# Second MLP's down projection: seven half-size block products per 1024-row group in place of eight

## The chip, the core and the metric

The kernel runs on one core of a Trainium2 chip. The core has five engines that work side by side, each through its own instructions in a fixed order: TensorE (PE in the profile, with PEld for the loading of its stationary operand), VectorE (DVE), ScalarE (ACT), GpSimd (POOL) and SyncE (SP, which here only issues transfers). They wait for each other by semaphores. Sixteen DMA engines move data between the device's memory and the on-chip memory; they are told what to do through queues that SP, ACT or POOL fill.

The metric is the time of one execution on the device, in microseconds (us). The time before is 1501.96 us, the median of three runs (1501.39 to 1502.55). The profile is one further execution, recorded instruction by instruction.

## What is computed

The reference is a two-layer decoder trunk over 512 positions of width 1024, in float32. A layer is a token mixer (a gated delta rule in the first, a convolution module in the second), a cross-attention, and an MLP. The change touches the MLP of the second layer and the final norm behind it; w_up is 1024 x 4096 and w_down 4096 x 1024:

```python
def sq_relu_mlp(h, w_up, w_down):
    return jnp.square(jax.nn.relu(h @ w_up)) @ w_down
...
        h = h + sq_relu_mlp(rms_norm(h, mlp_norm[layer]), mlp_w_up[layer], mlp_w_down[layer])
    return rms_norm(h, final_norm)
```

## The kernel before

Every projection runs in three passes: an operand x is split into a rounded part xh and the rest xl = x - xh, both of type float32r (fp32r in the profile), and a product is xh·wh + xl·wh + xh·wl (`mm3`, lines 236 to 240). One matmul instruction has a stationary operand of 128x128 and a moving one of 128x512.

**Weights.** They are read in halves of 128x1024, 512 KB each, in one long list (`order`) laid down beforehand for the whole kernel by `plan`. `wload` (line 197) issues the next half on SP's queue into a buffer `raw` (3 of them); `wsplit` (line 205) makes `wh` on ScalarE (line 214) and `wl` on VectorE (line 69, called from line 219), into 3 buffers each (`NW`); `wnext` (line 226) keeps loads and splits ahead of the use and hands out the next half. A third buffer of `wh` comes free when TensorE has finished the half three before. So the split of a half can run while TensorE works on the two halves before it.

**The MLP** (`mlp`, line 1008) goes through `MLP_ORDER`: up projections of 1024 hidden channels ("up", g) and down projections of the same channels ("dn", g), g from 0 to 3, the down projection one group behind the up projection. A step of either kind is 8 output tiles, each 24 matmuls (8 contraction tiles, three passes) on one weight half, into one of 8 PSUM banks. After an up tile VectorE makes `rl` (line 72: relu and the norm's factor), ScalarE squares it (line 1018) and `split` (line 275) makes `uh` and `ul`. After a down tile VectorE adds the bank to the running residual `h`. Activations lie with channels on the partitions, so `h` has 8 tiles of 128 channels x 512 positions.

**The last group** of the second MLP is done otherwise (`finish`, line 1497): for each of 4 blocks of 128 positions and each half of the channels one bank takes four transposes of the residual (line 1507) and 24 matmuls with the weights as the moving operand (lines 1510 to 1512), so that the output comes out with positions on the partitions. The final norm follows bank by bank: a square with a sum (ACT, line 1514), for the second half of a row block a square root (ACT, line 1523), a reciprocal (DVE, line 1524), a scaling of the first half (ACT, line 1525) and of the second (DVE, line 1526, profile line 72), and the two stores.

In the second layer's convolution GpSimd adds up taps (`cb`) and makes some `wl` itself, and VectorE runs a long series of taps over tiles `x7`, which lie in a pool `fsp` of 3 buffers of 128x1024.

Of the kernel before, what the change touches and what calls it, by code (L numbers as in the profile page):

```python
# [8 lines left out]
F32 = mybir.dt.float32  # L9
# [28 lines left out]
def tile_trunk(ctx, tc, xT, memT, x_d, mem_d, prm_d, adt_d, bdw_d, tap_d, fin_d, w_ab, w_kq, w_v, w_z, w_dno, w_pw1, w_pw2,  # L38
# [13 lines left out]
    def nm(s):  # L52
        cnt[0] += 1
        return f"{s}_{cnt[0]}"
# [4 lines left out]
    def psum(s="ps"):  # L59
        return psp.tile([P, NT], F32, tag="ps", name=nm(s))  # L60
# [42 lines left out]

    raw0 = wp.tile([P, 1024], F32, tag="raw", name="raw0", bufs=NRAW)

# [38 lines left out]

    order, srcs = [], {}

    def plan(key, src, n=2):
        srcs[key] = src
        for hf in range(n):
            order.append((key, hf))  # L150

# [12 lines left out]

    def plan_mlp(layer, last=False):
        for kind, g in MLP_ORDER:
            if last and (kind, g) == ("dn", 3):
                break
# [16 lines left out]
    for kind, i in CONV_SEQ:  # L185
        if kind == "p":
            order.append((("pw1", i // 2), i % 2))
        elif kind == "k":
            order.append((("K", 1, i // 2) if i < 8 else ("V", 1, i // 2 - 4), i % 2))
    for i in range(4):  # L190
        plan(("pw2", i), w_pw2[i])
    plan_x(1)
    plan_mlp(1, True)

    ws = {"next": 0, "split": 0, "load": 1, "raw": {0: raw0}, "hl": {}}

    def wload():
        u = ws["load"]
        key, hf = order[u]
        ws["load"] += 1  # L200
        raw = wp.tile([P, 1024], F32, tag="raw", name=nm("raw"), bufs=NRAW)
        nc.sync.dma_start(out=raw, in_=srcs[key][:, hf * 1024:(hf + 1) * 1024])
        ws["raw"][u] = raw

    def wsplit():
        u = ws["split"]
        ws["split"] += 1
        while ws["load"] <= u:
            wload()
        raw = ws["raw"].pop(u)  # L210
        h = wp.tile([P, 1024], F32R, tag="wh", name=nm("wh"), bufs=NW)
        lo = wp.tile([P, 1024], F32R, tag="wl", name=nm("wl"), bufs=NW)
        with tc.issue_after(ws["rb"].ins) if u == 4 else nullcontext():
            ins = [act.copy(h, raw)]  # L214
        if u < 4:
            tc.keep_in_program_order(ins[0])
        (kind, i, *j), hf = order[u]
# [6 lines left out]
        ws["hl"][u] = (h, lo)  # L224

    def wnext(key, hf):
# [7 lines left out]
        return ws["hl"].pop(i)  # L234

    def mm3(ps, wk, xk, first, last):
# [770 lines left out]

    def mlp(layer, norm, hres, nxt, mid=None, end=None, pre=None):
        xs = norm.xs
# [11 lines left out]
        for kind, g in MLP_ORDER:  # L1021
            if (kind, g) == ("dn", 3) and mid is not None:
                mid()
            if (kind, g) == ("dn", 3) and end is not None:
                return end(hid[3], cur)
            for i in range(8):
# [11 lines left out]
                else:  # L1038
                    proj(w, hid[g], ps)
                    if pre is not None and (g, i) in PRE:  # L1040
                        pre()
                    hn = slot(s="h")
# [444 lines left out]

    LAST = ((0, 0), (1, 0), (0, 1), (1, 1), (2, 0), (2, 1), (3, 0), (3, 1))
    ws_ = []

    def load():
        for m in range(2):
            raw = wp.tile([P, 1024], F32, tag="raw", name=nm("raw"), bufs=NRAW)
            nc.sync.dma_start(out=raw, in_=w_dn[1, 12 + len(ws_) // 4][:, m * 1024:m * 1024 + 1024])
            ws_.extend([split(raw[:, q * 512:(q + 1) * 512], "wd") for q in range(2)])

    def finish(hid, cur):
        gt = fsp.tile([P, 1024], F32, tag="fs", name=nm("gt"))
        nc.sync.dma_start(out=gt, in_=fin_d.partition_broadcast(P))
        st = {}  # L1500
        for c, g in LAST:
            if len(ws_) < 16:
                load()
            cs, gs = slice(c * P, (c + 1) * P), slice(g * 512, g * 512 + 512)
            ps = psum("dn")
            for j in range(4):
                pe.matmul(ps[:, j * P:(j + 1) * P], cur[4 * g + j][:, cs], ident, is_transpose=True, start=j == 0, stop=False)
            for k in range(KT):
                (xh, xl), (h, lo) = hid[k], ws_[8 * g + k]
                pe.matmul(ps, xh[:, cs], h, start=False, stop=False)  # L1510
                pe.matmul(ps, xl[:, cs], h, start=False, stop=False)
                pe.matmul(ps, xh[:, cs], lo, start=False, stop=k == KT - 1)
            ss, y = small(1), slot(s="y")
            act.activation(slot(s="fq"), ps, AF.Square, accum_out=ss)
            if g == 0:
                b = small(1)
                ts(dve, b, ss, 1.0 / 1024, ALU.mult, EPS, ALU.add)
                tt(dve, y, ps, gt[:, gs], ALU.mult)
                st[c] = y, b
                continue  # L1520
            y0, b = st.pop(c)
            sd, rc = small(1), small(1)
            act.activation(sd, ss, AF.Sqrt, bias=b, scale=1.0 / 1024)
            dve.reciprocal(rc, sd)
            act.activation(y0, y0, AF.Copy, scale=rc)
            stt(y, ps, rc, gt[:, gs], ALU.mult, ALU.mult)
            (act if c == 3 else nc.sync).dma_start(out=yT[cs, 0:512], in_=y0)
            nc.sync.dma_start(out=yT[cs, 512:1024], in_=y)

    mlp(1, n5, h, None, None, finish, load)  # L1530

# [3 lines left out]
NRAW = 3  # L1535
PRE = ((2, 4), (2, 6))
DN_ORDER = (("k", 0), ("q", 0), ("z", 0), ("v", 0), ("k", 1), ("q", 1), ("z", 1), ("v", 1))
# [75 lines left out]
def _layout(np, i):  # L1613
# [3 lines left out]
    def vec(v):  # L1617
# [31 lines left out]
    r["w_o"] = np.stack([_pack_a(np, i["xa_w_o"][j]) for j in range(2)])  # L1649
    r["w_up"] = np.stack([_pack_a(np, i["mlp_w_up"][j]) for j in range(2)])  # L1650
    r["w_dn"] = np.stack([np.concatenate([(_pack_b if (j, g) == (1, 3) else _pack_a)(
        np, i["mlp_w_down"][j][g * 1024:(g + 1) * 1024]) for g in range(4)]) for j in range(2)])
# [18 lines left out]
```

## Time and profile before

| what | value |
|---|---|
| median of 3 runs | 1501.96 us |
| span of the profiled execution | 1500.9 us |
| TensorE busy | 1492.3 us, 7458 matmuls |
| VectorE busy | 894.9 us |
| ScalarE busy | 685.1 us |
| GpSimd busy | 212.2 us |
| bytes moved by DMA | 155.65 MB |

The span runs from the first to the last recorded instruction; the time of a run also holds what lies around it. Busy time of an engine is the union of its instructions. Matmuls overlap each other in the record (a mean of 389 ns for one, while one starts every 227 ns in a dense stretch), so the pace of TensorE is read from stretches, not from the mean of one. Idle time of an engine is given with the instruction that ended it.

### The profile page before, as it was taken

How to read it: one execution, taken by the hardware profiler on the slowest of the kernel's cores; microseconds unless marked ns; L12 is line 12 of the kernel's file. 1: busy time of each engine (PE TensorE's matmuls, PEld its weight loads, DVE VectorE, ACT ScalarE, POOL GpSimd, SP SyncE). 2: the span in 40 equal slices, each digit the busy share in tenths (PEclk: the TensorE clock that was granted, in tenths of full speed). 3: DMA queues.
4: the chain of work that ended last, by engine and by line, in shares of the span. 5: the costliest groups of instructions: out<-in, count | busy, mean ns of one | idle time of the engine just before them, and what ended most of it. 6: DMA issues, size and time to landing. Idle time of an engine off the chain costs nothing.

```text
span 1500.9 us, 19205 instructions
## 1 busy us (share of the span) xinstructions
PE 1492.3 (99%) x7458; PEld 1258.5 (84%) x7458; DVE 894.9 (60%) x1318; ACT 685.1 (46%) x1202; POOL 212.2 (14%) x223
## 2 busy tenths in 40 slices
PE   9999999999999999999999999999999999999998
PEld 7888889888888888888888889988888888888886
DVE  6889888867555543444445799976555543434441
ACT  7856765555444432322324464564444431423332
POOL 1411311102111000000002496211111000000000
PEclk9999999999999999999999999999999999999999
DMA  6231223522212332222233524532122222232321
GB/s 240 83 120 57 68 88 113 174 94 88 79 48 96 99 98 98 98 99 97 92 123 130 190 88 140 170 123 98 57 71 90 93 98 98 98 98 99 98 99 56
DMA packets 50059, 155.65 MB, mean 104 GB/s; under 512 B 6320, under 2 KB 8624, under 8 KB 49968
## 3 DMA queue, kind: packets, MB, share of 16 engines
q1 hardware_dynamic: 49536, 153.90, 30.7%
q8 instruction: 58, 0.95, 0.3%
q10 hardware_dynamic: 432, 0.52, 0.1%
q14 instruction: 33, 0.27, 0.1%
HBM read 151.52 MB, written 2.10 MB: 102 GB/s over the span
## 4 chain that ended last, share of the span: by engine, by line
PE 96%; ACT 2%; DVE 1%; issue 0%; DMA 0%; POOL 0%; SPq 0%; DVEq 0%
PE up L238 8%; PE up L240 8%; PE up L239 8%; PE dn L240 7%; PE dn L238 7%; PE dn L239 7%; PE pw L240 3%; PE pw L239 3%; PE pw L238 3%; PE h L238 3%; PE h L239 2%; PE h L240 2%; PE xo L239 2%; PE q L238 2%; PE xo L240 2%; PE q L240 2%
## 5 line engine op out<-in xcount | busy, mean ns | idle before, releaser
L214 ACT CAST wh<-raw 128x1024 fp32r<-128x1024 f32 x247 | 259.2, 1051 | 598.1 <-PE dn L239 190.4
L69 DVE TENSOR_TENSOR wl<-raw,wh 128x1024 fp32r<-128x1024 f32 (+1 forms) x238 | 290.9, 1224 | 82.9 <-ACT wh L214 76.7
L240 PE MATMUL up<-xh,wl 128*128 128x512 f32 x512 | 199.2, 389 | 0.0
L239 PE MATMUL up<-xl,wh 128*128 128x512 f32 x512 | 199.2, 389 | 0.0
L238 PE MATMUL up<-xh,wh 128*128 128x512 f32 x512 | 199.2, 389 | 0.0
L240 PE MATMUL dn<-uh,wl 128*128 128x512 f32 x448 | 174.3, 389 | 0.0
L238 PE MATMUL dn<-uh,wh 128*128 128x512 f32 x448 | 174.3, 389 | 0.0
L239 PE MATMUL dn<-ul,wh 128*128 128x512 f32 x448 | 174.3, 389 | 0.0
L69 DVE TENSOR_TENSOR h<-dn,h 128x512 f32<-128x512 f32 x56 | 41.8, 747 | 165.3 <-PE dn L240 165.3
L72 DVE SCALAR_TENSOR_TENSOR rl<-up,rb 128x512 f32<-128x512 f32 x64 | 44.2, 691 | 153.8 <-PE up L240 153.7
L69 POOL TENSOR_TENSOR sq<-sq,sq 128x512 f32<-128x512 f32 x30 | 49.3, 1644 | 485.9 <-ACT sq L331 475.6
L240 PEld LDWEIGHTS up<-xh,wl 128*128 128x128 f32 x512 | 96.1, 188 | 20.0
L239 PEld LDWEIGHTS up<-xl,wh 128*128 128x128 f32 x512 | 96.1, 188 | 20.0
L238 PEld LDWEIGHTS up<-xh,wh 128*128 128x128 f32 x512 | 96.1, 188 | 19.9
L239 PEld LDWEIGHTS dn<-ul,wh 128*128 128x128 f32 x448 | 84.1, 188 | 17.6
L240 PEld LDWEIGHTS dn<-uh,wl 128*128 128x128 f32 x448 | 84.1, 188 | 17.4
L238 PEld LDWEIGHTS dn<-uh,wh 128*128 128x128 f32 x448 | 84.1, 188 | 17.4
L1148 DVE SCALAR_TENSOR_TENSOR ca<-x,prm,ca 128x512 f32<-128x512 f32 x112 | 82.3, 752 | 3.6 <-ACT ca L1145 1.3
L238 PE MATMUL h<-xh,wh 128*128 128x512 f32 x184 | 73.7, 400 | 0.0
L240 PE MATMUL h<-xh,wl 128*128 128x512 f32 x184 | 71.9, 391 | 0.0
L239 PE MATMUL h<-xl,wh 128*128 128x512 f32 x184 | 71.7, 390 | 0.0
L72 DVE SCALAR_TENSOR_TENSOR cva<-cv,prm,cva 128x512 f32<-128x512 f32 x60 | 48.3, 830 | 11.5 <-POOL cva L69 10.3
(364 smaller groups left out, 3037.4 us busy)
## 6 DMA issues: line engine op xcount, KB each, us to landing
raw<-w_up SPq DMA_DIRECT2D x64, 512.0 KB, 3.5
raw<-w_dn SPq DMA_DIRECT2D x64, 512.0 KB, 3.4
raw<-w_pw SPq DMA_DIRECT2D x24, 512.0 KB, 3.5
raw<-w_k SPq DMA_DIRECT2D x16, 512.0 KB, 3.6
raw<-w_vv SPq DMA_DIRECT2D x16, 512.0 KB, 3.6
raw<-w_q SPq DMA_DIRECT2D x16, 512.0 KB, 3.3
raw<-w_o SPq DMA_DIRECT2D x16, 512.0 KB, 3.6
raw<-w_kq SPq DMA_DIRECT2D x15, 512.0 KB, 3.6
```

The source lines that it names most:

```text
L69: return e.tensor_tensor(out=o, in0=a, in1=b, op=op)
L72: return dve.scalar_tensor_tensor(out=o, in0=a, scalar=s, in1=b, op0=op0, op1=op1)
L214: ins = [act.copy(h, raw)]
L238: pe.matmul(ps, wh, xh, start=first, stop=False)
L239: pe.matmul(ps, wh, xl, start=False, stop=False)
L240: pe.matmul(ps, wl, xh, start=False, stop=last)
L1148: first["tap"] = dve.scalar_tensor_tensor(out=a, in0=src, scalar=w, in1=a, op0=ALU.mult, op1=ALU.add)
```

## The change

It replaces `mlp` for the second layer (and `finish` with it) by `mlp7`.

- Within one group of 1024 hidden channels the down projection is a product of 512 positions x 1024 channels with 1024 channels x 1024 outputs. Each of the three sizes is cut in two, and the eight products of half blocks become seven products of sums and differences of blocks (Winograd's form of Strassen's scheme). A product is 2 blocks of 128 positions (c) x 4 contraction tiles x 3 passes = 24 matmuls of 128x128 by 128x512, with activations stationary and weights moving; it reads two weight halves of 128x1024, so that a half now feeds 12 matmuls and a group has 14 of them.
- The sums of weight blocks (T3, T1, T2, T4) are formed in the buffers by DMA: after a plain load from SP a second transfer, issued by GpSimd, adds another block to the same buffer (`more`). T3 and T1 are one load and one added block each. T2 is T1 plus a further block, added when T1 has been split; T4 is T2 plus another, added when T2 has been split. T1, T2 and T4 share a pair of buffers of `fsp`.
- The sums and differences of activations are made by VectorE after each up tile (`early`, `late`), in halves of 256 positions, and split.
- The outputs are kept in 8 running tiles of 128 positions x 512 channels and two sets of partial sums, `acc`; the residual is transposed into the eight in the first group (`turn`), and every product is added from its bank. In the last group the partial sums are distributed and the final norm follows (`final`).
- The groups run up 0, down 0, up 1, down 1, and so on. `raw` gets 6 buffers, the scratch space for descriptors of GpSimd's DMAs is made smaller, and the host lays out the weights accordingly.

```diff
+    base7, sums7 = {}, set()
+
+    def block(layer, g, b, h):
+        return w_dn[layer, g * 4 + BLOCKS7.index(b)][:, h * 1024:(h + 1) * 1024]
+
+    def plan_mlp7(layer):
+        for g in range(4):
+            for i in range(4):
+                plan(("up", layer, g * 4 + i), w_up[layer, g * 4 + i])
+            n, base7["u", g] = len(loads), len(order)
+            for b, h in LOADS7:
+                if b == "T1":
+                    sums7.add(len(loads))
+                loads.append([block(layer, g, c, h) for c in PARTS7.get(b, [b])])
+            for u in range(14):
+                order.append((("dn7", g), u))
+                bh = (ORDER7[u // 2][1], u % 2)
+                need.append(n + LOADS7.index(bh) if bh in LOADS7 else need[-1])
...
+        src = loads[u]
+        raw = fsp.tile([P, 1024], F32, tag="fs", name=nm("t")) if u in sums7 else raw_tile()
+        nc.sync.dma_start(out=raw, in_=src[0])
+        for a in src[1:]:
+            more(raw, a)
         ws["raw"][u] = raw
+
+    def more(t, a):
+        nc.gpsimd.dma_start(out=t, in_=a, accum_op=ALU.add)
...
-        while ws["load"] <= u:
+        while ws["load"] <= need[u]:
             wload()
-        raw = ws["raw"].pop(u)
+        (kind, i, *j), hf = order[u]
+        raw = combos7(1, i, hf) if kind == "dn7" else ws["raw"].pop(need[u])
...
-        while ws["load"] < min(i + NRAW + 2, len(order)):
+        while ws["load"] <= need[min(i + NRAW + 1 + 2 * (i > base7["u", 0] - 8), len(order) - 1)]:
...
+    def combos7(layer, g, u):
+        name, h = ORDER7[u // 2][1], u % 2
+        if name in ("T2", "T4"):
+            return T7[h]
+        t = ws["raw"].pop(need[u + base7["u", g]])
+        if name == "T1":
+            T7[h] = t
+        return t
+
+    def after7(layer, g, u):
+        name, h = ORDER7[u // 2][1], u % 2
+        if name in ("T1", "T2"):
+            more(T7[h], block(layer, g, "22" if name == "T1" else "21", h))
...
+    def mlp7(layer, norm, hres):
+        xs = norm.xs
+        acc, first = {}, []
+        gt = []
+
+        def turn(i):
+            n, m, c = i // 4, i // 2 % 2, i % 2
+            ps, a = psum("hT"), slot(s="acc")
             for j in range(4):
+                pe.transpose(ps[:, j * P:(j + 1) * P], hres[4 * m + j][:, n * 256 + c * P:n * 256 + c * P + P], ident)
+            act.copy(a, ps)
+            acc[n, m, c] = a
...
+        def early(o, u0):
+            tt(dve, u0[:, 256:512], u0[:, 256:512], u0[:, 0:256], ALU.subtract)
+            o["11"], o["R3"] = pair(split(u0, "a"))
+
+        def late(o, u0, u1):
+            x, y, r = slot(s="s12"), slot(s="s4"), slot(F32R, "s4")
+            tt(dve, x[:, 256:512], u1[:, 256:512], u0[:, 256:512], ALU.subtract)
+            tt(dve, x[:, 0:256], u0[:, 0:256], x[:, 256:512], ALU.subtract)
+            o["S1"], o["R2"] = pair(split(x, "s"))
+            o["12"], o["22"] = pair(split(u1, "a"))
+            tt(dve, y[:, 0:256], u1[:, 0:256], x[:, 256:512], ALU.subtract)
+            act.copy(r[:, 0:256], y[:, 0:256])
+            tt(dve, r[:, 256:512], y[:, 0:256], r[:, 0:256].bitcast(F32), ALU.subtract)
+            o["S4"] = [r[:, 0:256], r[:, 256:512]]
...
+            def part(left, w, ps, c, h, opens):
+                for kk in range(2):
+                    k, s = 2 * h + kk, slice(kk * 512, kk * 512 + 512)
+                    xh, xl = [t[:, c * P:(c + 1) * P] for t in ops[k][left]]
+                    pe.matmul(ps, xh, w[0][:, s], start=opens and k == 0, stop=False, skip_group_check=True)
+                    pe.matmul(ps, xl, w[0][:, s], start=False, stop=False, skip_group_check=True)
+                    pe.matmul(ps, xh, w[1][:, s], start=False, stop=k == 3, skip_group_check=True)
+
+            def product(i):
+                left, right, key, opens = ORDER7[i]
+                if opens:
+                    bank[key] = [psum("dn") for _ in range(2)]
+                ws_ = [wnext(("dn7", g), 2 * i)]
+                if (g, i) == (3, 6):
+                    ws_.append(wnext(("dn7", g), 13))
+                    todo = [(0, 0), (0, 1), (1, 0), (1, 1)]
+                else:
+                    todo = [(0, 0), (1, 0), (0, 1), (1, 1)]
+                for c, h in todo:
+                    if h == len(ws_):
+                        ws_.append(wnext(("dn7", g), 2 * i + 1))
+                    part(left, ws_[h], bank[key][c], c, h, opens)
+                    if h == 1:
+                        evict(right, c, bank[key][c])
+
+            def into(key, c, ps, op=ALU.add):
+                k = key + (c,)
+                if k not in acc:
+                    acc[k] = slot(s="acc")
+                    act.copy(acc[k], ps)
+                else:
+                    tt(dve, acc[k], acc[k], ps, op)
+                return acc[k]
...
+            def evict(right, c, ps):
+                last = g == 3
+                if right == "11":
+                    m = into(("m",), c, ps)
+                    if last:
+                        into((0, 0), c, m)
+                        into(("b",), c, m, ALU.subtract)
+                elif right == "T3":
+                    into((0, 1), c, ps, ALU.subtract)
+                elif right == "T1":
+                    into((1, 1), c, ps)
+                elif right == "21":
+                    into((0, 0), c, ps)
+                    if last:
+                        final(0, 0, c, True)
+                elif right == "T2":
+                    b = into(("b",), c, ps)
+                    if last:
+                        into((1, 1), c, b)
+                        final(1, 1, c, True)
+                        into((0, 1), c, b)
+                        into((1, 0), c, b, ALU.subtract)
+                elif right == "22":
+                    into((0, 1), c, ps)
+                    if last:
+                        final(0, 1, c, False)
+                else:
+                    into((1, 0), c, ps)
+                    if last:
+                        final(1, 0, c, False)
...
+        def final(n, m, c, opens):
+            x = acc[n, m, c]
+            rows = slice(n * 256 + c * P, n * 256 + c * P + P)
+            gs = slice(m * 512, m * 512 + 512)
+            ss = small(1)
+            act.activation(slot(s="fq"), x, AF.Square, accum_out=ss)
+            if opens:
+                b, y = small(1), slot(s="y")
                 ts(dve, b, ss, 1.0 / 1024, ALU.mult, EPS, ALU.add)
+                tt(dve, y, x, gt[0][:, gs], ALU.mult)
+                fin[n, c] = y, b, slice(m * 512, m * 512 + 512)
+                return
+            y1, b, gs1 = fin.pop((n, c))
+            sd, rc, y = small(1), small(1), slot(s="y")
             act.activation(sd, ss, AF.Sqrt, bias=b, scale=1.0 / 1024)
             dve.reciprocal(rc, sd)
+            act.activation(y1, y1, AF.Copy, scale=rc)
+            stt(y, x, rc, gt[0][:, gs], ALU.mult, ALU.mult)
+            (act if (n, c) == (1, 1) else nc.sync).dma_start(out=yT[rows, gs1], in_=y1)
+            nc.sync.dma_start(out=yT[rows, gs], in_=y)
...
+RAWB = 6
+BLOCKS7 = ["11", "21", "12", "22"]
+PARTS7 = {"T3": ["12", "22"], "T1": ["12", "11"]}
+LOADS7 = [(_b, _h) for _b in ("11", "T3", "T1", "21", "22") for _h in range(2)]
+ORDER7 = [("11", "11", "a", True), ("R3", "T3", "b", True), ("S1", "T1", "c", True), ("12", "21", "d", True),
+          ("R2", "T2", "b", False), ("S4", "22", "c", False), ("22", "T4", "e", True)]
...
+    halves = [8 * g + m for g in range(4) for m in (0, 4, 1, 5, 2, 6, 3, 7)]
+    r["w_up"] = np.stack([_pack_a(np, i["mlp_w_up"][j], halves if j else None) for j in range(2)])
+    r["w_dn"] = np.stack([np.concatenate([(_pack_b if j else _pack_a)(
         np, i["mlp_w_down"][j][g * 1024:(g + 1) * 1024]) for g in range(4)]) for j in range(2)])
...
+    nc = _bacc.Bacc("TRN2", target_bir_lowering=False, num_devices=1, dynamic_dma_scratch_size=1024)
```

More of the change, by code (lines that the diff above doesn't have):

```diff
@@ L149, in plan @@
         for hf in range(n):
-            order.append((key, hf))
+            put(key, hf)
     def plan_kv(layer, lo=0, hi=8):
@@ L1021, in mlp @@
         for kind, g in MLP_ORDER:
[L1022 removed]
+            if (kind, g) == ("dn", 3):
                 mid()
[L1024 to L1025 removed]
             for i in range(8):
@@ L1533 @@
+    mlp7(1, n5, h)
 NSLOT = 69
```

108 lines of the change are left out of this document (53 added, 55 removed).

## The prediction

> **What bounds the kernel now.** I read the page first: engines, clock, the chain that ended last.
>
> ```profile
> span 1500.9 us, 19205 instructions
> PE 1492.3 (99%) x7458; PEld 1258.5 (84%) x7458; DVE 894.9 (60%) x1318; ACT 685.1 (46%) x1202; POOL 212.2 (14%) x223
> PEclk9999999999999999999999999999999999999999
> q1 hardware_dynamic: 49536, 153.90, 30.7%
> PE 96%; ACT 2%; DVE 1%; issue 0%; DMA 0%; POOL 0%; SPq 0%; DVEq 0%
> ```
>
> TensorE is busy for 99% of the span and makes 96% of the chain, at an undisturbed clock. A matmul less is worth its pace, until another engine becomes late. So I cut the second MLP into stretches: both first up phases, dn 0, the four phases up to the last group, the last group. Columns are length, then busy time of each engine.
>
> ```profile
> 1142.33:1229.87 87.54, 87.54 (x388) 72.45 (x386) 45.69 (x51) 38.32 (x52) 0.00 (x0) 1.00 0.28 96
> 1229.87:1273.39 43.52, 43.52 (x194) 36.04 (x192) 15.99 (x17) 9.58 (x11) 0.00 (x0) 1.00 0.29 97
> 1273.39:1447.64 174.25, 174.25 (x771) 144.26 (x770) 74.02 (x86) 56.66 (x74) 0.00 (x0) 1.00 0.31 103
> 1447.64:1500.90 53.26, 47.35 (x224) 38.88 (x222) 12.18 (x25) 11.65 (x28) 0.00 (x0) 0.97 0.13 50
> ```
>
> A phase has 192 matmuls by the code (the counts hold neighbours cut by the edge). The second row gives 43.52/192 = 0.2267 us for one, without a gap. VectorE, third number, is busy for 37% of a down phase, and there is room. GpSimd does nothing here. In the last row TensorE ends 47.35 us in, at 1495.0; 5.9 us of tail follow. The groups of instructions in this MLP give the prices (busy us, mean ns of one):
>
> ```profile
> L69 DVE TENSOR_TENSOR wl<-raw,wh 128x1024 fp32r<-128x1024 f32 x54 | 66.2, 1225 | 14.5 <-ACT wh L214 14.5
> L214 ACT CAST wh<-raw 128x1024 fp32r<-128x1024 f32 x54 | 56.9, 1053 | 188.4 <-PE up L239 94.7 <-PE dn L239 87.5 <-issue 6.1
> L1510 PE MATMUL dn<-wdh,uh 128*128 128x512 f32 x64 | 25.7, 401 | 0.0
> L69 DVE TENSOR_TENSOR ul<-u,uh 128x512 fp32r<-128x512 f32 x32 | 22.1, 692 | 2.8 <-ACT uh L277 2.7
> L72 DVE SCALAR_TENSOR_TENSOR rl<-up,rb 128x512 f32<-128x512 f32 x32 | 22.1, 691 | 76.9 <-PE up L240 76.8
> L1018 ACT ACTIVATE u<-rl 128x512 f32<-128x512 f32 x32 | 20.0, 626 | 3.3 <-DVE rl L72 3.3
> L277 ACT CAST uh<-u 128x512 fp32r<-128x512 f32 x32 | 19.9, 622 | 1.0
> L69 DVE TENSOR_TENSOR h<-dn,h 128x512 f32<-128x512 f32 x24 | 16.6, 691 | 73.8 <-PE dn L240 73.8
> L1507 PE MATMUL dn<-ident,h 128*128 128x128 f32 x32 | 4.8, 272 | 0.0
> ```
>
> **TensorE's sum.** A group falls from 192 to 168 matmuls, four groups by 96. Activations stationary and weights moving is the form of the last group today (L1510), whose mean of 401 ns against 389 elsewhere comes from the first one behind each set of transposes; the pace is the same. 96 x 0.2267 = 21.8 us. Transposes stay 32 (4.8 us), moved from the last group into up 0. Had every other thing its cover, the span would be 1500.9 - 21.8 = 1479.1.
>
> **Splits.** A down phase now splits 14 halves in 168 x 0.2267 = 38.1 us, one every 2.72 us instead of 5.44. ScalarE needs 1.05 us of these, VectorE 1.22, and VectorE adds 14 banks of 0.69: 14 x 1.91 = 26.8 us, 70% of the phase. In an up phase it has per pair of tiles 2 x (1.22 + 0.69) plus about 4 us for sums, differences and three splits (0.69 each, half-size ones estimated at 0.4), 8 of 10.9 us. That is hidden as long as nothing stands wrongly in its queue, so I followed the queues in the built order. At the turn from up to down the worst case is the half of T1 (unit 4, counting the 14 halves from 0): ScalarE cannot take unit 3's half before unit 0's buffer is free, 2.72 + 1.05 = 3.8 us into the phase; from there VectorE has in order that split (1.22), two low parts of the last pair and a bank (3 x 0.69), a half-size difference, a bank, a half-size low part (0.4 + 0.69 + 0.4) and T1's split (1.22), ready at 9.8. Unit 4 starts at 4 x 2.72 = 10.9. No stall, 1.1 us to spare.
>
> **Last group: VectorE's queue.** Here each product's bank is not only added but distributed. Product 4 (T2) ends on its first position block at 25.8 us of the phase; from there VectorE's queue holds, in order, eight additions of 0.69, two products with the gain of 0.68, three splits of 1.225 and two tiny ones (0.15): 10.9 us, and the split of the very last half is the last of them, ready at 36.7. Product 6 begins at 12 x 2.72 = 32.6 and, in the order given for it alone, wants that half's low part after 8 matmuls, at 34.4. TensorE stalls for 36.7 - 34.4 = 2.2 us (1.5 if neighbours overlap by the 0.05 us that such rows do).
>
> **Tail.** Before, one chain follows the last matmul:
>
> ```profile
> 1495.03 0.60 ACT L1514 ACTIVATE fq<-dn 128x512 f32<-128x512 f32 x1 [5.22 <-PE dn L1512]
> 1495.53 0.19 ACT L1514 ACTIVATION_READ_ACCUMULATOR fq<-dn 128x1 f32 x1
> 1495.75 0.29 ACT L1523 ACTIVATE sm<-sm,sm 128x1 f32<-128x1 f32 x1
> 1496.08 0.16 DVE L1524 RECIPROCAL sm<-sm 128x1 f32<-128x1 f32 x1 [5.49 <-ACT sm L1523]
> 1496.28 0.72 ACT L1525 ACTIVATE y<-y,sm 128x512 f32<-128x512 f32 x1 [0.23 <-DVE sm L1524]
> 1496.35 0.75 DVE L72 SCALAR_TENSOR_TENSOR y<-dn,sm,gt 128x512 f32<-128x512 f32 x1
> 1497.12 0.33 SPq L1528 DMA_DIRECT2D yT<-y  x1
> ```
>
> From 1495.0 to 1497.1 it computes; 3.8 us more are the store and the end. After, four such chains are left at the end, and their instructions stand interleaved: the reciprocal of row block 1 is queued on VectorE behind the very last bank's addition, ScalarE's scaling waits for that reciprocal, and the squares of blocks 2 and 3 wait behind the scaling. From the last matmul on: addition 0.69, reciprocal 0.16, scaling 0.72, then square, sum and root (0.60 + 0.19 + 0.29), reciprocal, scaling, again square, sum and root, reciprocal, and 0.75: 0.69 + 3 x 0.16 + 2 x 0.72 + 2 x 1.08 + 0.75 = 5.5 us against 2.1. That adds 3.4 us, 0.7 at the least (the new addition alone).
>
> **The accumulating DMAs** are what the trace does not show. The nearest rows are a plain load of the same size from SP and, above, that queue's share: 0.307 x 1500.9 us of all 16 engines for 153.90 MB, 1.57 us for 512 KB.
>
> ```profile
> raw<-w_dn SPq DMA_DIRECT2D x27, 512.0 KB, 3.5
> ```
>
> So 3.5 us to landing is 1.57 of transfer and 1.9 of issue and completion. From below, an addition costs the engines no more than a plain load. From above I take three times that, as it reads both sources and writes one: 3 x 1.57 + 1.9 = 6.6 us, 11.3 for the second of two that queue. GpSimd's own issue is unpriced too. The deadlines: T1's first half has been split at 9.8, T2 must have landed by 19.5, to be split (2.3) when unit 8 starts at 21.8; the second half, from 11.1 to 22.2; T4, from 18.7 to 30.4. At the upper price T2's halves land at 16.4 and 21.1, T4's after 18.7 + 6.6 = 25.3. No stall at either end; I take 0. T3 and T1 themselves are added many units ahead. The Trainium skill, page "Collectives: The Full Stack", section on why ReduceScatter is half of AllGather, says that an inline add costs two source reads on one ring and nothing for the add; by it, estimated, a load of 1.57 becomes 3.1 us and T2 lands earlier than above. No run here shows it.
>
> **Moved transfers.** T1's loads for groups 0 and 1 and three additions are drawn forward into the convolution, where `fsp` comes free. On SP they wait for taps that end before the next weight's own buffer is free, so nothing behind them is held. On GpSimd two additions stand between `cb` and `wl`:
>
> ```profile
> 925.05 2.63 POOL L69 TENSOR_TENSOR cb<-cb,cvp 128x512 f32<-128x512 f32 x2 [3.02 <-ACT cvp L1162]
> 933.92 2.39 POOL L69 TENSOR_TENSOR wl<-raw,wh 128x1024 fp32r<-128x1024 f32 x1 [6.24 <-ACT wh L214]
> 938.36 7.58 POOL L69 TENSOR_TENSOR cb<-cb,cvp 128x512 f32<-128x512 f32 x5 [2.04 <-ACT cvp L1162]
> 947.71 2.41 POOL L69 TENSOR_TENSOR wl<-raw,wh 128x1024 fp32r<-128x1024 f32 x1 [1.77 <-ACT wh L214]
> ```
>
> GpSimd idles 6.2 and 1.8 us there, so an issue of up to 1.8 us is free; if it takes longer, the second `wl` and a key projection are late by the excess, a microsecond or so. I take 0. The other edits (6 buffers, other host layouts) issue nothing new.
>
> **The sum.** 1500.9 - 21.8 + 2.2 + 3.4 = 1484.7 of span. Runs lie 1502.0 - 1500.9 = 1.1 above the profiled span, so the forecast is 1485.8, say 1486, 1.1% faster.
>
> **Rivals.**
> (A) The additions are slow. What decides is s, the time that one takes of the DMA engines: T2's halves land at 11.7 + s and 11.7 + 2s and must by 19.5 and 22.2, so the stall begins at s = 5.2. At s = 6 it is 1.5 us for T2 and 1.1 for T4 behind it, 10 us in four groups: 1496. At s = 8 it is 10.6 per group and 42 in all: 1528, slower. It breaks even near s = 6.4, four times a plain load of 1.57. For it: nothing like it is in the trace, and ScalarE's queue stops behind a late T2. Against: four times a plain load is beyond every byte that it moves. A loss so made has 0.14, a gain shrunk by it to between 1490 and 1500.5, 0.12.
> (B) The new work on VectorE and ScalarE stalls TensorE at each turn from up to down as well: the 1.1 us to spare is gone if the half-size operations take 0.69 like full ones and each wait between engines adds 0.1 to 0.2. Then about 1 us per group: 1490. The first two rows of groups speak against it (0.69 for 512, 1.22 for 1024: length counts). 0.08.
> (C) The queues at the end do not bind, since the store of the earlier rows is long done and neighbours overlap: only 0.7 of tail. 1500.9 - 21.8 + 0.7 + 1.1 = 1480.9. The built order speaks against it. 0.08.
> (D) The matmuls saved come back as pauses at weight changes, or the products are paced by loads: no change, 1501 to 1503. The third row of the stretches, 31% DMA share without a gap, speaks against it. 0.03.
>
> **How the numbers follow.** Forecast 0.55, and with (A)'s shrunk gain, (B) and (C) the kernel is faster by over 0.2% (3 us, about what a measurement can tell) with 0.83; within 0.2% 0.03; slower 0.14. The range runs from (C), 1480, to 1498, which holds (B) and (A) up to s of about 6; what is left out is (A) beyond.
>
> **What would show it.** Right: 96 matmuls less, up phases of 43.5 us, down phases of 38.1 with TensorE without a gap in groups 0 to 2, additions that land in 4 to 7 us, a gap of about 2 us before the last 10 to 16 matmuls with VectorE's `wl` as releaser, and some 9.3 us from the last matmul to the end. Wrong: ScalarE's `wh` from T2 or T4 waiting for a DMA and TensorE behind it; gaps at the first matmuls with S1; `wl` on GpSimd late in the convolution.

## The result and the profile after

The changed kernel takes 1487.01 us (median of 4 runs, 1485.96 to 1487.96) against 1502.19 (4 runs) before: a ratio of 0.9899, 95% interval 0.9885 to 0.9913. Two further sets of four runs gave 1485.70 (ratio 0.9888, 0.9873 to 0.9903) and 1485.35 (0.9885, 0.9871 to 0.9900). The forecast was 1486. The profiled execution spans 1486.0 us. Its page, with span, engines, GpSimd's DMA queue and the shares of the chain that ended last:

```profile
span 1486.0 us, 19375 instructions
PE 1472.0 (99%) x7362; PEld 1241.1 (84%) x7362; DVE 986.7 (66%) x1468; ACT 729.0 (49%) x1262; POOL 240.2 (16%) x255
q0 software_dynamic: 4608, 16.78, 6.6%
PE 94%; DVE 3%; ACT 2%; issue 1%; DMA 1%; POOL 0%; SPq 0%; DVEq 0%
```

TensorE still bounds the kernel, with 96 matmuls less. VectorE got 92 us more to do, nearly all under TensorE's cover. The second MLP by stretches, up and down in turn (length, busy time of PE, PEld, DVE, ACT and POOL, granted clock, DMA share, GB/s):

```profile
1145.16:1192.81 47.65, 47.65 (x228) 39.55 (x226) 33.34 (x48) 26.80 (x40) 1.78 (x2) 1.00 0.41 111
1192.81:1231.00 38.19, 38.19 (x172) 31.62 (x170) 25.21 (x29) 18.91 (x25) 5.17 (x6) 1.00 0.70 179
1231.00:1274.52 43.52, 43.52 (x194) 36.04 (x192) 27.79 (x43) 18.97 (x29) 1.75 (x2) 1.00 0.59 157
1274.52:1312.60 38.08, 38.08 (x170) 31.53 (x168) 28.26 (x34) 16.74 (x19) 5.21 (x6) 1.00 0.71 180
1312.60:1356.12 43.52, 43.52 (x194) 36.04 (x192) 27.78 (x43) 18.98 (x29) 1.74 (x2) 1.00 0.58 158
1356.12:1394.20 38.08, 38.08 (x170) 31.53 (x168) 28.35 (x34) 16.74 (x19) 4.35 (x5) 1.00 0.70 181
1394.20:1437.72 43.52, 43.52 (x194) 36.04 (x192) 27.79 (x43) 18.97 (x29) 1.76 (x2) 1.00 0.51 144
1437.72:1485.98 48.26, 38.29 (x169) 31.27 (x167) 38.11 (x59) 23.91 (x40) 3.48 (x4) 0.94 0.38 88
```

In the first seven rows the second number equals the first: TensorE has no gap at any turn. A down phase is 38.1 us where a phase of 192 matmuls takes 43.5. The DMA share, 0.31 over the four phases shown of before, is 0.70 in the down phases, without a visible price. In the last row TensorE works 38.29 us and then the tail follows.

The balance of the two profiles has three lines. From the start of the second MLP to the end of the last matmul: 1494.99 - 1142.33 = 352.66 before, 1476.01 - 1145.16 = 330.85 after, -21.8. From there to the end: 5.9 before, 1485.98 - 1476.01 = 9.97 after, +4.1. The start of that MLP: 1142.33 before, 1145.16 after, +2.8. Sum: -14.9, as the spans say. The third line was not in the forecast. It has two halves. One lies in the first 14 us of the kernel, where the change touches nothing:

```profile
0.00:14.00 14.00, 11.55 (x41) 8.20 (x42) 7.02 (x13) 8.43 (x15) 2.45 (x19) 0.88 0.88 284
```

The granted clock is 0.88 there and 41 matmuls have started; before, it was 1.00 and 47. The single matmuls of that stretch:

```profile
8.29 0.58 PE L1392 MATMUL h<-xh,wh 128*128 128x512 f32 x1 [1.01 <-ACT xh L372]
8.67 0.63 PE L1393 MATMUL h<-xh,wl 128*128 128x512 f32 x1
9.10 0.63 PE L1395 MATMUL ab<-xh,abp 128*32 128x512 f32 x1
...
11.65 0.55 PE L1396 MATMUL h<-xl,wh 128*128 128x512 f32 x1
12.04 0.40 PE L1399 MATMUL ab<-xl,abp 128*16 128x512 f32 x1
```

From 8.67 on they start every 0.43 us instead of 0.23, for eight matmuls, 1.6 us in all; from 12.0 us on TensorE is 1.45 us behind the profile of before. The Trainium skill, page "TensorE: Matmul & The Clock Gate", Part 1, puts the start of a matmul of 512 columns at every 0.427 us while the gate halves the clock after idling; the pace in the trace agrees. What set the slow clock off is not shown: TensorE had been idle for 1.01 us just before, and as long in an execution of the same kernel at full clock. The other half, 1.3 us, is a gap in the second layer's convolution. GpSimd's timeline there (start, duration, engine, line, operation; in brackets the idle time before and what seems to have ended it):

```profile
939.84 6.21 POOL L69 TENSOR_TENSOR cb<-cb,cvp 128x512 f32<-128x512 f32 x4 [2.06 <-ACT cvp L1206]
951.07 0.88 POOL L233 DMA_DIRECT2D t<-w_dn  x1 [5.02 <-DVE ca L1192]
951.68 1.60 POOL L69 TENSOR_TENSOR cb<-cb,cvp 128x512 f32<-128x512 f32 x1
952.94 2.65 POOL L69 TENSOR_TENSOR wl<-raw,wh 128x1024 fp32r<-128x1024 f32 x1
```

its plain load on SP's queue, the times to landing of the transfers of `t` between 930 and 957 us, and the matmul that follows on TensorE:

```profile
942.31 0.38 SPq L227 DMA_DIRECT2D t<-w_dn  x1
...
DMA to landing us min/median/max: 5.3/5.8/8.2
...
955.64 0.39 PE L288 MATMUL K<-mh,wl 128*128 128x256 f32 x1 [1.14 <-POOL wl L69]
```

One of the additions drawn forward (L233) waits for 5.0 us on GpSimd. VectorE's `ca`, which the row names, had been done; a plain load of `t` issued at 942.31 took 8.2 us to land, at 950.5, behind three weight loads, and the addition was issued 0.55 us later. One addition to `cb` and `wl` stand behind it, and a key projection on TensorE waits for that `wl`.

The tail, by ScalarE's timeline:

```profile
1474.02 0.63 ACT L1648 ACTIVATE fq<-acc 128x512 f32<-128x512 f32 x1 [2.88 <-DVE acc L69]
...
1475.48 0.72 ACT L1659 ACTIVATE y<-y,sm 128x512 f32<-128x512 f32 x1 [0.40 <-DVE sm L1658]
1476.11 0.61 ACT L1648 ACTIVATE fq<-acc 128x512 f32<-128x512 f32 x1
...
1478.00 0.61 ACT L1648 ACTIVATE fq<-acc 128x512 f32<-128x512 f32 x1
...
1479.89 0.61 ACT L1648 ACTIVATE fq<-acc 128x512 f32<-128x512 f32 x1
...
1481.15 0.72 ACT L1659 ACTIVATE y<-y,sm 128x512 f32<-128x512 f32 x1 [0.23 <-DVE sm L1658]
```

Four chains, one behind the other: the second square starts 2.09 us behind the first, the next two 1.89 us apart. Each square stands in ScalarE's queue behind the scaling of the chain before it. The first starts at 1474.0, before the last matmul has ended at 1476.0.

### The profile page after: what moved, and what is told of

The parts are those of the page before. It is cut to its first block, busy times and chain, and to the rows that moved or that the text cites. A ratio compares the mean times of both kernels' runs of the same rounds, so it can differ in the third digit from the quotient of the medians.

```text
span 1486.0 us, 19375 instructions
## 1 busy us (share of the span) xinstructions
PE 1472.0 (99%) x7362; PEld 1241.1 (84%) x7362; DVE 986.7 (66%) x1468; ACT 729.0 (49%) x1262; POOL 240.2 (16%) x255
## 4 chain that ended last, share of the span: by engine, by line
PE 94%; DVE 3%; ACT 2%; issue 1%; DMA 1%; POOL 0%; SPq 0%; DVEq 0%
PE up L288 8%; PE up L287 8%; PE up L286 8%; PE dn L287 4%; PE dn L288 4%; PE dn L286 4%; PE dn L1578 3%; PE dn L1579 3%; PE dn L1577 3%; PE pw L288 3%; PE pw L287 3%; PE pw L286 3%; PE h L286 3%; PE h L287 2%; PE h L288 2%; PE xo L287 2%
## 5 line engine op out<-in xcount | busy, mean ns | idle before, releaser
L245 ACT CAST wh<-raw 128x1024 fp32r<-128x1024 f32 x255 | 267.7, 1051 | 498.1 <-PE up L287 133.7
L69 DVE TENSOR_TENSOR wl<-raw,wh 128x1024 fp32r<-128x1024 f32 (+1 forms) x246 | 303.7, 1236 | 93.7 <-ACT wh L245 87.6
L72 DVE SCALAR_TENSOR_TENSOR rl<-up,rb 128x512 f32<-128x512 f32 x64 | 44.2, 691 | 106.0 <-PE up L288 105.9
L286 PE MATMUL dn<-uh,wh 128*128 128x512 f32 x256 | 99.6, 389 | 0.0
L287 PE MATMUL dn<-ul,wh 128*128 128x512 f32 x256 | 99.6, 389 | 0.0
L288 PE MATMUL dn<-uh,wl 128*128 128x512 f32 x256 | 99.6, 389 | 0.0
L69 DVE TENSOR_TENSOR h<-dn,h 128x512 f32<-128x512 f32 x32 | 25.2, 788 | 91.5 <-PE dn L288 91.5
L286 PEld LDWEIGHTS dn<-uh,wh 128*128 128x128 f32 x256 | 48.0, 188 | 10.1
L287 PEld LDWEIGHTS dn<-ul,wh 128*128 128x128 f32 x256 | 48.0, 188 | 9.9
L288 PEld LDWEIGHTS dn<-uh,wl 128*128 128x128 f32 x256 | 48.0, 188 | 9.9
```

The costliest lines, as they stand in the source:

```text
L69: return e.tensor_tensor(out=o, in0=a, in1=b, op=op)
L72: return dve.scalar_tensor_tensor(out=o, in0=a, scalar=s, in1=b, op0=op0, op1=op1)
L286: pe.matmul(ps, wh, xh, start=first, stop=False)
L287: pe.matmul(ps, wh, xl, start=False, stop=False)
L288: pe.matmul(ps, wl, xh, start=False, stop=last)
```

## The experiments

**A plain copy in place of each addition.**

```diff
-        nc.gpsimd.dma_start(out=t, in_=a, accum_op=ALU.add)
+        nc.gpsimd.dma_start(out=t, in_=a)
```

> Each addition becomes a plain copy of the same block into the same buffer, issued by the same GpSimd instruction (the sums of weight blocks are left out, so the outputs are others). Theory: an addition costs the DMA engines a second read, so GpSimd's queue falls from 25.5% of the engines in the second MLP (3.04 us for 512 KB) to about 1.57 us for 512 KB, 13%, and issue to landing from 5.3-5.7 us to about 4; the waits are the same, so the time stays within 1 us of 1487 and the down phases at 38.1. Rival: the price is GpSimd's own making of descriptors, then landing stays above 5 us and the share above 20%.

1484.53 us (one run). GpSimd's queue in the second MLP, changed kernel first (packets, MB, share of 16 engines), and its transfers of `t` (count, KB each, median us to landing):

```profile
q0 software_dynamic: 4176, 15.21, 25.5%
...
t<-w_dn POOLq DMA_DIRECT2D x21, 512.0 KB, 5.6
```

With plain copies:

```profile
q0 software_dynamic: 4176, 15.21, 12.9%
...
t<-w_dn POOLq DMA_DIRECT2D x21, 512.0 KB, 4.0
```

These windows are 346 us long and 15.21 MB are 29 halves: 0.255 x 346 / 29 = 3.04 us of all engines for an addition, 0.129 x 346 / 29 = 1.54 for a copy, a factor of 1.97. The price is paid in the DMA engines. The rule of two source reads (the Trainium skill, page "Collectives: The Full Stack", why ReduceScatter is half of AllGather) gave an estimated 3.1; the runs agree. Down phases stay at 38.1, and from the start of the second MLP to the end it is 340.80 us against 340.82, so neither price is on the path. The time lies 2.5 us below 1487, outside the 1 us expected, because the second MLP began earlier (1141.86).

**No additions at all.**

```diff
     def more(t, a):
-        nc.gpsimd.dma_start(out=t, in_=a, accum_op=ALU.add)
+        pass
```

> All additions of weight blocks are left out (the outputs are others); loads and products stay. Theory: the additions cost nothing in the second MLP, and 1.4 us in the convolution, where one of them holds GpSimd while it waits for VectorE: the second MLP begins 1.4 us earlier, down phases stay at 38.1, time 1485.6. Rival: the additions cost nothing anywhere (1487 +- 0.5, second MLP at the same start, so the 1.4 us come from the earlier plain loads); or they also slow the down phases by sharing the DMA engines (more than 2.5 us gained).

1484.83 us (4 runs, 1484.22 to 1486.95), ratio 0.9882 (0.9865 to 0.9898). The gap in the convolution is gone, and the down phases are those of the changed kernel again. The second MLP began at 1144.23, 0.9 earlier than in the first profile of the changed kernel, though the 61st matmul of this execution started 0.5 later (18.99 against 18.50): some 1.4 us regained, the size of the gap. In the second MLP only the last stretch differs, 48.05 against 48.26. The expectation had GpSimd waiting for VectorE; by the landing above it waits for the load. One profile without a gap shows little by itself, since the changed kernel has executions without one too (below).

**T2's and T4's additions doubled.**

```diff
-            more(T7[h], block(layer, g, "22" if name == "T1" else "21", h))
+            more(T7[h], block(layer, g, "22" if name == "T1" else "21", h))
+            more(T7[h], block(layer, g, "22" if name == "T1" else "21", h))
```

> Each addition that makes T2 and T4 is issued twice, the second behind the first (one block is added twice, so the outputs are others). By the deadlines of the prediction and the landings measured (T2's first half issued 9.9 us into a down phase, 5.3 us to landing) the extra lands at about 20.6 against 19.5, the second half at 27-31 against 22.2, and T4's second half again 1-5 us late: 6 to 14 us a group, 24 to 56 in all, time 1511 to 1543, with ScalarE's wh waiting for a DMA and TensorE behind it. Rival: the additions have so much room that doubling them is hidden too: 1487.

1534.07 us (one run). Down phases 0 to 2 and the last one with its tail, by stretches:

```profile
1190.34:1240.75 50.41, 42.42 (x171) 33.58 (x170) 24.84 (x29) 18.65 (x25) 8.14 (x10) 0.93 0.73 170
...
1284.27:1335.34 51.07, 43.55 (x169) 34.04 (x168) 28.13 (x34) 16.47 (x19) 8.71 (x10) 0.90 0.72 172
...
1378.86:1428.96 50.10, 42.23 (x169) 33.16 (x168) 26.43 (x33) 16.50 (x19) 7.85 (x9) 0.93 0.70 164
...
1472.48:1532.27 59.79, 42.67 (x169) 33.14 (x167) 38.20 (x59) 23.56 (x40) 6.96 (x8) 0.87 0.49 106
```

Each grew by 11.5 to 13.0 us, 48.8 in all, within the 6 to 14 per group expected. Waits in group 1 (who waited for whom, us in total, times, longest):

```profile
ACT wh L245 <- DMA t<-w_dn: 22.4, 4, 10.9
...
PEld dn L1578 <- ACT wh L245: 8.1, 2, 5.1
```

This is the chain of the prediction's rival (A), late addition, ScalarE's split, TensorE. The second addition to a buffer is issued when the first has landed, so that the two follow each other with their whole times to landing. Not all of the loss is waiting: of the 13.0 us by which this phase grew, TensorE is idle for 7.5, and its busy time grew by 5.5, since behind the two long waits its matmuls start every 0.43 us for a while (granted clock 0.90 over the phase). The deadlines are real, and one addition per buffer keeps them.

**The last product in the order that the prediction reckoned with.**

```diff
-                    part(left, ws_[h], bank[key][c], c, h, opens)
+                    with tc.issue_after(z.ins) if (g, i, c, h) == (3, 6, 1, 0) else nullcontext():
+                        z = part(left, ws_[h], bank[key][c], c, h, opens)
```

(`part` returns its last matmul.)

> In the very last product the six matmuls of the second position block are held behind the twelve of the first, the order the prediction reckoned with. Theory: TensorE then waits 1.2-1.3 us for the last low part (ready 35.7 us into the phase, wanted at 34.4), but the four chains of the final norm begin at VectorE's additions before it and set the end, so the time stays within 0.5 us of 1487. Rival (as in the prediction's sum): the stall and the tail add, +1.2 us or more on the profiled span behind the start of the last down phase (48.3 us becomes 49.5).

1485.36 us (one run). TensorE's timeline, and the stretch from the last down phase on, of this kernel:

```profile
1469.54 0.39 PE L1578 MATMUL dn<-wh,al 128*128 128x512 f32 x1
1471.04 0.50 PE L1579 MATMUL dn<-wl,ah 128*128 128x512 f32 x1 [1.11 <-DVE wl L69]
```

```profile
1435.31:1483.57 48.26, 38.54 (x169) 31.27 (x167) 38.10 (x59) 23.91 (x40) 3.48 (x4) 0.95 0.37 88
```

TensorE now loses 1.50 - 0.23 = 1.27 us in front of the last low part, and the stretch is 48.26 us, as without that loss. (The time is 1.6 us below 1487 because the second MLP began at 1142.75.) The stall and the tail don't add: the four chains set the end.

**The changed kernel again.**

> The changed kernel once more, beside the next three on the same chip: 1487 +- 1. Theory: of the 2.83 us that its second MLP began later in the first profile, the early 1.46 are chance (the clock in the first 14 us) and the convolution's 1.3 are half chance, so here the second MLP begins between 1142 and 1145.5, and the stretches behind that are again 47.65, 38.2, 43.5, 38.1, 43.5, 38.1, 43.5 and 48.3 to within 0.1. Rival: both losses belong to the change, and the second MLP begins at 1145 +- 0.3 again.

1485.70 us (4 runs, 1484.91 to 1486.05), and in a later set:

> The changed kernel beside it: 1486 +- 1; second MLP's stretches as in its first two profiles, 48.3 for the last with its tail, and a gap of 0 to 1.3 us in the convolution.

1485.35 us (4 runs, 1484.68 to 1485.54). The second MLP began at 1143.22 and 1142.86; behind that the eight stretches repeat to within 0.03 us (48.25 twice for the last). The clock in the first 14 us was 1.00 both times. The gap in the convolution was 0.8 us in the first of these and none in the second; there GpSimd's row names the wait directly:

```profile
947.79 0.88 POOL L233 DMA_DIRECT2D t<-w_dn  x1 [2.67 <-DMA t<-w_dn]
```

It waited 2.7 us for the load, not 5.0, and TensorE's cover sufficed. Of six profiles with the additions where the change puts them, two show the gap (1.3 and 0.8 us): both the start and the gap vary from one execution to the next, as the theory said. The six traces also settle the gap's cause. In each of them this addition is issued 0.55 us after its plain load has landed, whatever engine the row names, and the gap goes with the wait: GpSimd waited 5.0 and 4.5 us in the two with a gap, and 2.7 to 3.3 us in the other four (0.1 us lost at most).

**Additions held behind GpSimd's last `wl`.**

```diff
-        nc.gpsimd.dma_start(out=t, in_=a, accum_op=ALU.add)
+        with tc.issue_after(ws["gp"].ins):
+            nc.gpsimd.dma_start(out=t, in_=a, accum_op=ALU.add)
```

(`ws["gp"]` is the last `wl` made on GpSimd.)

> The additions of the first weight sums are held behind GpSimd's last wl of the convolution; all else as in the changed kernel. Theory: GpSimd no longer waits there for a load of T1, TensorE has no gap in the convolution, and 0 to 1.3 us are gained on average (1486.3); nothing in the first down phase is late by it (T1 still has over 200 us). Rival: the gap has another cause (the plain loads of T1 on SP's queue ahead of the value weights) and stays.

1484.88 us (4 runs, 1484.63 to 1485.13), ratio 0.9884 (0.9867 to 0.9900). GpSimd runs as before the change:

```profile
938.02 7.58 POOL L69 TENSOR_TENSOR cb<-cb,cvp 128x512 f32<-128x512 f32 x5 [2.03 <-ACT cvp L1209]
947.38 2.41 POOL L69 TENSOR_TENSOR wl<-raw,wh 128x1024 fp32r<-128x1024 f32 x1 [1.78 <-ACT wh L246]
949.73 1.97 POOL L234 DMA_DIRECT2D t<-w_dn  x2
```

There is no gap, here or in the three later profiles with this edit. The median is 0.8 us lower than that of the changed kernel beside it, but the ranges overlap (1484.91 to 1486.05 there), and a gap of about 1 us in a third of the executions would give 0.4. The traces show the gap gone; the times don't show the gain.

**One scaling moved, alone and with the edit before.** The first three of the four row blocks:

```diff
-            act.activation(y1, y1, AF.Copy, scale=rc)
+            if (n, c) == (1, 1):
+                act.activation(y1, y1, AF.Copy, scale=rc)
+            else:
+                ts(pool, y1, y1, rc, ALU.mult)
```

> For the first three of the last four row blocks the scaling of the first half goes to GpSimd (an estimated 1.3 us each, as its additions of that size), so that ScalarE does squares and roots alone. Theory: ScalarE's order is what spaces the four chains by 1.89 us; they then follow at 1.08, the last product with the gain ends at 41.7 to 42.0 us of the last phase instead of 43.5 (last phase with its tail 46.0 +- 0.3 instead of 48.3), time 1484.7. Rival: VectorE's additions and splits before them are the bound (gain under 0.5 us), or GpSimd slows VectorE beside it (VectorE's 0.75 us products take over 1).

1486.39 us (4 runs, 1485.73 to 1487.72): no gain; the last stretch is 48.64. With both edits:

> Both edits together (additions behind, scaling on GpSimd). Theory: the gains add, 2.3 + 0 to 1.3: 1484.0 +- 0.8, faster than the changed kernel by about 3 us. Rival: as each alone.

1485.32 us (4 runs, 1485.19 to 1486.16): no gain either, last stretch 48.65. The theory was right in its place and failed at the end: ScalarE's squares did follow at 0.94 us, and ScalarE and VectorE ended 42.0 us into the phase instead of 44.2. But GpSimd took 1.85 us on average for a scaling, not 1.3 (its row in the run with this edit alone):

```profile
1474.34 5.55 POOL L76 TENSOR_SCALAR y<-y,sm 128x512 f32<-128x512 f32 x3 [15.03 <-DVE sm L1658]
```

It ended at 1479.9, 1.4 us behind ScalarE and VectorE, and the last stores stood behind its own in SP's queue.

**One scaling on GpSimd, three on ScalarE behind the last root.**

```diff
+            if (n, c) == (0, 0):
+                first()
+            else:
+                held.append(first)
+            if (n, c) == (1, 1):
+                with tc.issue_after(root.ins):
+                    for f in held:
+                        f()
```

(`first` scales the first half, on GpSimd for row block 0, and stores it.)

> As the run with both edits, but GpSimd scales only the first of the four row blocks (it took 1.85 us there for one, not 1.3), and ScalarE scales the other three behind the last root; SP's stores of these stand behind the stores of the products with the gain. Theory: the arithmetic ends 42.2 us into the last phase as before, no store waits for GpSimd any more, and 4.1 us later is the end: last phase with its tail 46.3 instead of 48.3, time 1483.5 to 1484. Rival: the stores themselves bind, eight of 256 KB at 0.79 us of all engines each (half of 1.57) from the first one at 38.6 on, 6.3 us and 2 to complete: 46.9 at the least, time 1484.2 or more.

1484.81 us (4 runs, 1484.30 to 1486.25). The last stretch is 48.0, not 46.3: the rival was right, and the stores bind. The busy share of the DMA engines over the last 12 us, in 40 slices, tenths each:

```profile
DMA  0000000000000000499999999999999999400000
```

One unbroken block, 2.10 MB at some 380 GB/s, 5.5 us: the arithmetic ends at 1476.3, and the engines drain until 1481. The changed kernel, over its last 13 us, shows four shorter blocks with rests, one for each chain:

```profile
DMA  0000000000004999706999508999409999200000
```

**The early row blocks early.** From this reading: nothing on GpSimd, four operations of VectorE that only row blocks 2 and 3 need moved behind the additions of product 5 (the sixth, counted from 0), scalings of row blocks 0 and 1 behind the second root. The additions of weights stay behind GpSimd's last `wl`, as in the two runs before this one with that edit.

```diff
-                        final(1, 1, c, True)
+                        later.append(final(1, 1, c, True))
                         into((0, 1), c, b)
-                        into((1, 0), c, b, ALU.subtract)
+                        later.append(lambda: into((1, 0), c, b, ALU.subtract))
...
                         final(0, 1, c, False)
+                        while c and later:
+                            later.pop(0)()
...
+            held.append(first)
+            if c == 1:
+                with tc.issue_after(root.ins):
+                    while held:
+                        held.pop(0)()
```

> No work on GpSimd in the tail; four operations of VectorE that only the last two row blocks need (two products with the gain, two additions to partial sums) are moved behind the additions of the sixth product; ScalarE scales row blocks 0 and 1 behind the second root and 2 and 3 behind the last one; each product with the gain is stored ahead of the scaled half; additions of weights behind the convolution. Theory: what binds in the run before is the stores, 2.10 MB at about 380 GB/s in 5.7 us from the first of them on (37.0 to 37.7 after the last matmul's 38.3 there); here the square of row block 0 starts at 33.7 to 34.5 of the last phase instead of 36.3, its stores go out from about 36 on, arithmetic ends at 42.0 as before, the last four stores need 2.9 us from 41 on and 1.3 to complete: the last phase with its tail is 46.0 to 46.5 instead of 48.0 to 48.3, time 1483.3. Rival: the end is set by the last chain and what lies behind a store whatever goes out before it, 48.0 again.

1483.28 us (4 runs, 1482.31 to 1484.00), ratio to the kernel before 0.9874 (0.9858 to 0.9891). All four runs lie below the twelve of the changed kernel (1484.68 to 1487.96). Its last stretch, and its DMA strip over the last 13 us:

```profile
1434.89:1480.94 46.05, 38.24 (x169) 31.34 (x167) 37.82 (x59) 23.71 (x40) 3.48 (x4) 0.97 0.37 92
```

```profile
DMA  0000000000001999979997000397699999700000
```

46.05 us, 2.2 less than the changed kernel, within the 46.0 to 46.5 expected: half of the stores are out before the last chains end. The arithmetic ends 42.0 us into the phase here, as it did with scalings on GpSimd (last stretch 48.65) and with one scaling there (48.0). So the 2 us between these runs lie in the stores. The edit of the additions alone left the last stretch at 48.25.

## Why the prediction was right, and where its steps were not

**TensorE's sum** held to the digit: 21.8 us by 96 x 0.2267, and 21.8 in the balance. No rival (D).

**Splits** held. T1's first half was to be ready 9.8 us into the phase; GpSimd's first addition to T2, which waits for that, starts at 1284.38, 9.86 into down 1. VectorE was to be busy for 26.8 us of a down phase and was so for 25.2 to 28.4. No gap at a turn, so no rival (B).

**The accumulating DMAs** cost 3.04 us of the engines, between the bounds 1.57 and 4.7, and nothing on the path, as taken. Doubled, one behind the other, they lose some 12 us per group: the chain of rival (A) exists, and what kept it away is the price, which is not four times but twice that of a plain load.

**Last group, VectorE's queue.** Here the step failed. The last low part was ready at 1473.39, 35.7 us into the phase where 36.7 was reckoned, but TensorE lost less than 0.1 us instead of 2.2. VectorE's last split and the additions behind it, and TensorE's timeline in the last product, which begins at 1470.36:

```profile
1472.17 1.22 DVE L69 TENSOR_TENSOR wl<-t,wh 128x1024 fp32r<-128x1024 f32 x1
1473.30 2.06 DVE L69 TENSOR_TENSOR acc<-acc,dn 128x512 f32<-128x512 f32 x3
...
1471.94 0.39 PE L1578 MATMUL dn<-wh,al 128*128 128x512 f32 x1
1472.17 0.39 PE L1577 MATMUL dn<-wh,ah 128*128 128x512 f32 x1
...
1473.31 0.64 PE L1579 MATMUL dn<-wl,ah 128*128 128x512 f32 x2
```

The prediction took the order in which the code writes these matmuls, by which a product with the low part (L1579) follows at 1472.17. In the built order six matmuls of the second position block stand there, so that the first to want that low part comes at the 15th place and not the 9th; it is the second of the last row, at 1473.5. With the order reckoned there is a loss of 1.27 us, and it changes nothing: 2.2 and 3.4 should not have been added, since the chains of the tail start from VectorE's additions and not from the last matmul. The first square (1474.02) waits for an addition that stands behind that same split.

**Tail.** The mechanism was right, the four interleaved chains and each square behind a scaling. The size was short, 4.1 us more instead of 3.4. When the last matmul ended, three chains were still whole to come, 3 x 1.89 = 5.7 and 5.9 measured, where 5.5 had the first of the three already past its root; and the end lies 4.1 us behind the last scaling instead of 3.8. Rival (C), queues that don't bind, was wrong for the kernel as built.

**Moved transfers.** The step priced what GpSimd spends on issuing (free up to 1.8 us; it takes 0.9 to 1.05) and not the wait in front of it: the addition can't be issued until its own plain load has landed, and it holds what stands behind it on GpSimd. It costs 0 to 1.3 us by the execution. Without it, or with the addition placed behind, there is no gap (five profiles). The prediction had named a late `wl` in the convolution as a sign that it is wrong, at a price of a microsecond or so; the sign came, by another way than the issue, and was small.

**The sum.** In the profiled execution the terms close: 1484.7 of span, less 2.1 for the stall that didn't come, plus 0.65 for the tail and 2.8 for the later start of the second MLP, make 1486.0. The step from span to time was short too: 1.1 was the median of the runs against the span of another execution, and this execution took 1487.96, 2.0 above its own span. So against 1487.01, 1485.70 and 1485.35 the large term was exact, and that 1486 lies so close is in part luck, since a stall 2.1 too long made up for terms that were too small. The first 50 us vary by more than any of these (below).

## What to carry to other kernels

Where a transfer that adds into a buffer is issued by an engine that also computes, price the wait for the buffer's first content, not only the issue, and place it behind that engine's urgent work. Read the order of the built queues also for the engine that is the bound, and don't add up stalls that end in the same chain. When the work behind the last matmul is cut, look at the stores next: here they drained at some 380 GB/s, and ending the arithmetic 2.2 us earlier gave 0.24 us at most, until the first stores went out earlier.

## What the runs showed of the hardware that was not expected

The same first instructions started TensorE at two paces. In two of the twelve profiles of kernels with the change's structure (the first, and the one without additions) the clock of the first 14 us was 0.88 instead of 1.00; the 61st recorded matmul starts there at 18.5 and 19.0 us, and at 15.9 to 17.3 in the others. The clock is not the whole of the spread: the profile with the scaling on GpSimd alone had 1.00 there, and waits before 48 us (0.85 us of them at 27.9) put it 1.5 us behind the profile of before, as far as the first. By the 201st recorded matmul the twelve lie between 46.75 and 49.20 us. In the changed kernel GpSimd issues an accumulating transfer in 0.86 to 1.05 us, and with plain copies in 0.53 to 0.78. Three scalings of a tile of 128x512 by a number per partition took GpSimd 1.55 to 2.05 us each, beside a busy VectorE. Its additions of two such tiles took 1.27 to 2.15 us, mostly 1.3, so the trace does not show which is slower by itself. During the scalings, in the run with that edit alone, one of VectorE's products of 0.75 us took 1.09:

```profile
1476.52 1.09 DVE L72 SCALAR_TENSOR_TENSOR y<-acc,sm,gt 128x512 f32<-128x512 f32 x1
```

Why was not tried.
